# Paired indexer heads, idle products in routing and in the last quarters, and 512-column squares in a one-core transformer block

## The chip, the core and the metric

The kernel runs on one core of a Trainium2 chip. Its engines work side by side and meet at semaphores: PE (TensorE, the matmuls; PEld is its weight loads), DVE (VectorE), ACT (ScalarE), POOL (GpSimd) and SP, which issues the DMAs that bring weights from HBM. The metric is the device time of one execution in microseconds (us).

## The reference, cut to what matters

One layer of 256 frames with 1024 channels: a norm, one wide projection, two attention branches, gates, an output projection, then a mixture of 32 experts and a final norm. Three pieces of it are touched. The **indexer** scores keys with 8 heads of 64 channels:

```python
logits = jnp.einsum('bqhd,bkd->bqhk', qii, k_idx).astype(jnp.float32) * (IDX_DIM ** -0.5)
score = jnp.einsum('bqh,bqhk->bqk', wi.astype(jnp.float32), jax.nn.relu(logits))
_, sel = lax.top_k(score, top_k)          # the keys that branch B attends to
```

The **experts** are 8 groups of 4; each frame goes to one group and two experts in it. The **final norm** closes the block:

```python
for e in range(N_EXPERTS):
    hid = jax.nn.silu(jnp.matmul(h, w_gate[e])) * jnp.matmul(h, w_up[e])
    out = out + jnp.matmul(hid, w_down[e]) * combine[:, e:e + 1]
...
return rmsnorm(x, final_norm_g)
```

## The kernel before, in words

The program is one straight line of stages. **Attention** (to about 218 us) streams 32 slabs of weights through a ring, splits each into a high and a low part on ACT and DVE (L282, L283, L297) and runs three products for each piece on PE (`mm3`, L301 to L303). Up to the output projection a scheduler sets each engine's order, with products of several stages woven into one another. The indexer's scores are made by `select(j)` for the two blocks of 128 queries: block 0 has 128 keys, block 1 has 256. Heads 0 to 3 lie in rows 0 to 63 of the operands, heads 4 to 7 in rows 64 to 127, so each product uses 64 rows of the array (shape 64\*128 in the profile). A bank of PSUM `s` holds 4 heads of block 0 or 2 of block 1; ACT takes the relu (L479), DVE the weighted sum (L482) and the top 64 (L486, L487).

**Routing** (218 to 229 us) and the **experts** (from 229 us) are written in the order in which they run. Routing makes the logits (L778), chooses experts on DVE (`chosen`, L792 to L810), counts places with small products (`cums`, L915, L916, L922), and gathers the tokens (L844). An expert group then takes 12 slabs of 1 MB: two for each expert (`gate_up`, L993) and four quarters of the down projection (`down`, L1030, 256 output channels each). `combine` weighs a result and splits it into `hi` (ACT) and `lo` (DVE), both L297, and its `scatter` adds them with four products (L1044) to the output banks `OA[t][h]`, t for the half of the frames, h for the half of the channels.

Weights of the experts go into some 24 places of SBUF; `take` issues the next DMA when the place's former holder has been used. In the last group (`grp == NG - 1`) `heat` puts idle bf16 products of the identity (L310) after some gate and up products, into a bank `idle_bank` that nobody reads.

The **last quarters** (q = 0 to 3 of the last group) run one by one: `down(q)` calls the scatter of quarter q-1 between its two halves, `combine(q)` follows. Quarters 0 and 1 share one bank of PSUM, 2 and 3 another. After quarter 2 the finished 512 channels are squared (ACT, L318) and multiplied by the norm's gain (DVE, L1112); after quarter 3 the channels 512 to 767 are; the last 256 follow behind the last scatter (L1176), then the roots, the scaling (L1183, L1184) and two DMAs out (L1185).

Of the kernel before, what the change touches and what calls it, by code (L numbers as in the profile page):

```python
# [25 lines left out]
HEAT = 4  # L26
# [52 lines left out]
def block_kernel(ctx: ExitStack, tc: tile.TileContext, a, out, cap=CAP):  # L79
    nc = tc.nc  # L80
# [230 lines left out]

    scr_turn = [0]
# [152 lines left out]
    def select(j):  # L465

        nk = 128 * (j + 1)
        per = 512 // nk
        qs = slice(j * 128, (j + 1) * 128)
        sc = e0[:, 1664:1920] if j else e0[:, 1536:1664]  # L470
        for h0 in range(0, 8, per):
            p = pss()
            for i in range(per):
                h = h0 + i
                ps_ = slice(64 * (h // 4), 64 * (h // 4) + 64)
                mm3(p[:, i * nk:(i + 1) * nk], qiT[ps_, 0, h % 4, qs], qiT[ps_, 1, h % 4, qs],
                    kiT[ps_, 0, :nk], kiT[ps_, 1, :nk], True, True)
            rl = wk.tile([128, 512], F32, tag="b2", name="rl", bufs=3)
            nc.scalar.activation(rl, p, AF.Relu)  # L479
            for i in range(per):  # L480
                h = h0 + i
                nc.vector.scalar_tensor_tensor(sc, rl[:, i * nk:(i + 1) * nk], wi[:, j, h:h + 1],  # L482
                                               adm[:, 256 - nk:] if h == 0 else sc, op0=ALU.mult, op1=ALU.add)
        for r in range(TOPK // 8):
            m8 = wk.tile([128, 8], F32, tag="m8", name="m8")
            nc.vector.max(out=m8, in_=sc)  # L486
            nc.vector.match_replace(out=sc, in_to_replace=m8, in_values=sc, imm_value=TAKEN)  # L487
        nc.vector.tensor_scalar(bias[:, j, :nk], sc, -2e38, NEG, op0=ALU.is_gt, op1=ALU.mult)
# [425 lines left out]
    residual(1)  # L914
    nc.tensor.matmul(cums[0][:, :NE], tri, sel[:, 0], start=True, stop=True)  # L915
    nc.tensor.matmul(cums[1][:, :NE], ones, sel[:, 0], start=True, stop=False)  # L916
    residual(2)
    residual(3)
    in_turn(chosen(1))
    in_turn(placed(0, cums[0][:, :NE]))  # L920
    gx = [pss("gx") for _ in range(2)]
    nc.tensor.matmul(cums[1][:, :NE], tri, sel[:, 1], start=False, stop=True)  # L922
    gather(0, 0, gx[0])
# [98 lines left out]
    def down(grp, q, w, between=None):  # L1022

        if q % 2 == 0:
            Ys[grp, q // 2] = pss("Y")
        Y = Ys[grp, q // 2][:, 256 * (q % 2):256 * (q % 2) + 256]
        wv = w.rearrange("p (f e c) -> p f e c", f=2, e=EPG)
        for f in range(2):
            for e in range(EPG):
                nc.tensor.matmul(Y[quarters[e]], hT_[:, e, f], wv[:, f, e], start=f == 0, stop=f == 1)  # L1030
            if f == 0 and between:
                between()

    def combine(grp, q0, n):
# [4 lines left out]
        evac_g(hi, lo, Ys[grp, h][:, c0:c0 + w], ws)  # L1039

        def scatter():
            for t in range(2):
                for v in (hi, lo):
# [70 lines left out]
    with in_order, tc.manual_schedule(engines={mybir.EngineType.Activation, mybir.EngineType.DVE}):  # L1114
# [42 lines left out]
        scatter = None  # L1157
        for q in range(4):
            down(grp, q, take()[1], scatter)
            scatter = combine(grp, q, 1)  # L1160
            if q == 2:
                for t in range(2):
                    final_part(t, 0, 512, 0)
            elif q == 3:
                for t in range(2):
                    final_part(t, 512, 256, 1)
                nc.vector.tensor_add(fs[:, :, 0], fs[:, :, 0], fs[:, :, 1])
                early = [early_root(fs[:, t, 0:1], D, f"nf{t}") for t in range(2)]
        scatter()
# [3 lines left out]
    with tc.manual_schedule(engines={mybir.EngineType.Activation, mybir.EngineType.DVE}):  # L1173
        cs = slice(768, 1024)
        for t in range(2):
            nc.vector.tensor_mul(ob[:, t, cs], OA[t][1][:, 256:], g_fin[0][:, cs])  # L1176
        roots = []
        for t in range(2):
            sumsq(OA[t][1][:, 256:], 256, fs[:, t, 2:3], scr[:, 2 * t + 1, 256:])
# [90 lines left out]
```

## Time and profile before

| | us |
|---|---|
| three timed runs | 435.72, 432.21, 435.73 (median 435.72) |
| the profiled execution, whole | 431.72 |
| its span, which all times of rows count from | 430.0 |
| PE busy | 397.2 (92%) |
| DVE busy / ACT busy | 206.7 / 184.6 |
| mean granted clock of TensorE over the span | 0.973 |
| DMA read from HBM | 133.36 MB |

All durations in the prediction come from the profiled execution. It stands 4.00 us under the median of the runs and 0.49 us under the fastest of them; the span leaves out 1.72 us of the whole. Views give the start and the duration of an instruction, and neighbours of one kind are merged into one line with a count (x4). Products overlap in the pipeline, so the distance from start to start says what one costs, not its duration. The granted clock is 1.00 at 2.4 GHz and 0.50 at 1.2 GHz.

### The profile page before, as it was taken

The numbers are of one execution on the slowest core, as the hardware profiler recorded it, in microseconds if no ns is written. First come the engines' busy times: TensorE is split into PE (matmuls) and PEld (weight loads), VectorE is DVE, ScalarE is ACT, GpSimd is POOL, SyncE is SP. The second block draws the span as 40 slices with busy tenths as digits, with TensorE's granted clock in tenths as the row PEclk, the third lists the DMA queues.
The fourth block names the chain that finished last, engine by engine and source line by source line (L and its number), as shares of the span: only waits on it lengthen the run. The fifth ranks groups of instructions, "written<-read, shape, count | busy, mean of one in ns | idle before, by whom it ended". The sixth has DMA issues, their size and how long they took to land.

```text
span 430.0 us, 8090 instructions
## 1 busy us (share of the span) xinstructions
PE 397.2 (92%) x3255; PEld 291.6 (68%) x3255; DVE 206.7 (48%) x547; ACT 184.6 (43%) x407; POOL 26.5 (6%) x30
## 2 busy tenths in 40 slices
PE   6999999999999999999989999999999798787760
PEld 3888878888867777888877757575757374364420
DVE  2899599989757464757563221221213011020033
ACT  4885586677756566565433122212221111120242
POOL 0870000000000000000001010101010101000000
PEclk9999999999999999999999999999999979699995
DMA  7985573648543456888994999999999999999952
GB/s 261 390 357 238 196 287 111 257 171 343 197 150 143 148 204 238 325 312 335 332 356 171 425 419 418 422 419 419 420 420 421 419 419 421 421 420 418 414 215 103
DMA packets 20638, 134.98 MB, mean 314 GB/s; under 512 B 2418, under 2 KB 2930, under 8 KB 5620
## 3 DMA queue, kind: packets, MB, share of 16 engines
q1 hardware_dynamic: 20596, 134.42, 79.1%
q8 instruction: 27, 0.44, 0.4%
q14 instruction: 15, 0.12, 0.1%
HBM read 133.36 MB, written 1.05 MB: 313 GB/s over the span
## 4 chain that ended last, share of the span: by engine, by line
PE 70%; DMA 24%; DVE 2%; ACT 1%; issue 0%; SPq 0%; DVEq 0%; ACTq 0%
DMA w<-in_w_moe 23%; PE a L301 13%; PE a L302 13%; PE a L303 12%; PE G L993 8%; PE gx L844 4%; PE Y L1030 3%; PE G L1009 2%; PE OA L1044 2%; PE o L595 2%; PE s L301 2%; PE t L583 1%; PE s L303 1%; PE s L302 1%; DMA w<-in_w_att 1%; PE t L532 1%
## 5 line engine op out<-in xcount | busy, mean ns | idle before, releaser
L302 PE MATMUL a<-r 128*128 128x512 f32 (+1 forms) x244 | 93.7, 388 | 0.0
L303 PE MATMUL a<-r 128*128 128x512 f32 (+1 forms) x244 | 91.9, 383 | 0.0
L301 PE MATMUL a<-r 128*128 128x512 f32 (+1 forms) x244 | 83.7, 387 | 1.0 <-ACT r L297 1.0
L993 PE MATMUL G<-w,tok 128*32 128x256 f32 x1024 | 70.0, 401 | 13.3 <-DMA w<-in_w_moe 13.3
L297 DVE SCALAR_TENSOR_TENSOR r<-w,ident,r 128x512 fp32r<-128x512 f32 (+2 forms) x79 | 62.0, 799 | 13.5 <-ACT r L297 13.3
L297 ACT ACTIVATE r<-w,ident 128x512 fp32r<-128x512 f32 (+2 forms) x79 | 56.6, 751 | 27.4 <-PE a L303 26.2
L993 PEld LDWEIGHTS G<-w,tok 128*32 128x32 f32 x1024 | 29.6, 113 | 39.8 <-issue 15.3
L302 PEld LDWEIGHTS a<-r 128*128 128x128 f32 x244 | 45.9, 188 | 8.6 <-DVE r L297 0.4
L301 PEld LDWEIGHTS a<-r 128*128 128x128 f32 x244 | 44.8, 188 | 10.3 <-ACT r L297 1.9
L303 PEld LDWEIGHTS a<-r 128*128 128x128 f32 x244 | 45.8, 188 | 8.3
L1015 DVE TENSOR_TENSOR P<-G,P 128x64 f32<-128x64 f32 x32 | 7.2, 225 | 82.7 <-ACT P L1014 82.7
L1014 ACT ACTIVATE P<-G 128x64 f32<-128x64 f32 x32 | 7.2, 224 | 75.1 <-PE G L1009 75.1
L1030 PE MATMUL Y<-w,P 128*32 128x256 f32 x512 | 30.5, 382 | 3.2 <-DVE ysb L297 2.2
L999 ACT COPY Gs<-G 128x256 f32<-128x256 f32 x32 | 11.9, 372 | 48.0 <-PE G L993 48.0
L844 PEld LDWEIGHTS gx<-Pr,x 128*128 128x128 f32 x256 | 29.8, 195 | 3.9 <-issue 3.3
L844 PE MATMUL gx<-Pr,x 128*128 128x128 f32 x256 | 31.4, 282 | 0.5 <-DVE Pr L829 0.5
L297 DVE SCALAR_TENSOR_TENSOR ysb<-Y,ws,ysb 128x512 fp32r<-128x512 f32 (+1 forms) x18 | 12.4, 691 | 37.6 <-ACT ysb L297 20.3
L283 DVE TENSOR_TENSOR r<-w,r 128x512 fp32r<-128x512 f32 x32 | 21.9, 690 | 16.7 <-ACT r L282 15.1
L829 POOL TENSOR_SCALAR Pr<-P,r 128x128 f32<-128x128 f32 x14 | 8.3, 607 | 323.5 <-PE gx L844 198.8
L282 ACT CAST r<-w 128x512 fp32r<-128x512 f32 x32 | 19.9, 624 | 14.6 <-PE a L303 9.5
L1030 PEld LDWEIGHTS Y<-w,P 128*32 128x32 f32 x512 | 15.4, 109 | 13.7 <-DVE ysb L297 3.2
L849 DVE TENSOR_TENSOR tok<-gx,ident 128x512 f32<-128x512 f32 x16 | 11.1, 692 | 27.4 <-PE gx L844 27.3
(211 smaller groups left out, 482.2 us busy)
## 6 DMA issues: line engine op xcount, KB each, us to landing
w<-in_w_moe SPq DMA_DIRECT2D x93, 1024.0 KB, 19.8
w<-in_w_att SPq DMA_DIRECT2D x24, 1024.0 KB, 4.9
w<-in_w_moe SPq DMA_DIRECT2D x6, 512.0 KB, 15.0
w<-in_w_att SPq DMA_DIRECT2D x3, 744.0 KB, 8.5
w<-in_w_att SPq DMA_DIRECT2D x2, 512.0 KB, 5.0
out<-r SPq DMA_DIRECT2D x2, 512.0 KB, 3.8
w<-in_w_att SPq DMA_DIRECT2D x1, 768.0 KB, 4.8
w<-in_w_att SPq DMA_DIRECT2D x2, 372.0 KB, 6.1
```

The costliest lines, as they stand in the source:

```text
L282: nc.scalar.copy(hi, src)
L283: nc.vector.tensor_sub(lo, src, hi.bitcast(F32))
L297: return nc.scalar.mul(hi, ps, g), nc.vector.scalar_tensor_tensor(lo, ps, g, hi.bitcast(F32), op0=ALU.mult, op1=ALU.subtract)
L301: i = nc.tensor.matmul(out_, lh, rh, start=start, stop=False)
L302: nc.tensor.matmul(out_, lh, rl, start=False, stop=False)
L303: nc.tensor.matmul(out_, ll, rh, start=False, stop=stop)
L595: nc.tensor.matmul(o[r, c * 256 + 128 * b:(c + 1) * 256], v[:, b, 64 * (4 * quad + h):][:, :64], PT[:, h, 0:2] if b == 0 else PT[:, h, 2], ...
L844: nc.tensor.matmul(p[:, kk * GRP:(kk + 1) * GRP], x2[:, t, k * 128:(k + 1) * 128], Pr[:, t], start=(t == 0 and kk == 0), stop=(t == 1 and ...
L849: nc.vector.tensor_mul(tokens[c], p.rearrange("p (k s) -> p k s", k=4), bc(g_ffn[:, 4 * c:4 * c + 4], GRP, axis=2))
L993: nc.tensor.matmul(G[quarters[2 * z + o], :256], tokens[c][:, kk + o, CAP * e:CAP * e + CAP], w[:, (kk + o) * 512 + z * 256:(kk + o) * 512 ...
L999: nc.scalar.copy(Gs, G[:, :256])
L1030: nc.tensor.matmul(Y[quarters[e]], hT_[:, e, f], wv[:, f, e], start=f == 0, stop=f == 1)
```

## The change

The change has five parts. (1) `select` makes the heads in pairs, one of each half of the rows, and its products alternate between the halves (`mm3_pair`); two banks are filled at once. (2) Routing gets 14 idle products (6, 5 and 3) into the unused columns of `lgp[0]`. (3) In the last four quarters each quarter has a bank of its own, and idle products stand in them: 5 ahead of each scatter, 2 behind each quarter, 10 more ahead of the last scatter; `HEAT`, the number used between gate and up products as well, goes from 4 to 5. (4) `scatter` runs both `hi` products first, then both `lo`. (5) The squares and gain products of channels 512 to 1023 are made in one piece behind the last scatter.

```diff
-HEAT = 4
+HEAT = 5
...
+    row_halves = slice(0, 64), slice(64, 128)
+    def mm3_pair(both, start, stop):
+        for l, r, s0, s1 in ((1, 3, start, False), (1, 4, False, False), (2, 3, False, stop)):
+            for ops in both:
+                nc.tensor.matmul(ops[0], ops[l], ops[r], start=s0, stop=s1)
...
-        for h0 in range(0, 8, per):
-            p = pss()
+        for h0 in range(0, 4, per):
+            p = [pss() for _ in range(2)]
             for i in range(per):
-                h = h0 + i
-                ps_ = slice(64 * (h // 4), 64 * (h // 4) + 64)
-                mm3(p[:, i * nk:(i + 1) * nk], qiT[ps_, 0, h % 4, qs], qiT[ps_, 1, h % 4, qs],
-                    kiT[ps_, 0, :nk], kiT[ps_, 1, :nk], True, True)
-            rl = wk.tile([128, 512], F32, tag="b2", name="rl", bufs=3)
-            nc.scalar.activation(rl, p, AF.Relu)
...
+                mm3_pair([(p[z][:, i * nk:(i + 1) * nk], qiT[ps_, 0, h0 + i, qs], qiT[ps_, 1, h0 + i, qs],
+                           kiT[ps_, 0, :nk], kiT[ps_, 1, :nk]) for z, ps_ in enumerate(row_halves)], True, True)
+            for z in range(2):
+                rl = wk.tile([128, 512], F32, tag="b2", name="rl", bufs=3)
+                nc.scalar.activation(rl, p[z], AF.Relu)
...
     residual(1)
+    heat(lgp[0], 6)
     nc.tensor.matmul(cums[0][:, :NE], tri, sel[:, 0], start=True, stop=True)
...
     residual(3)
+    heat(lgp[0], 5)
...
     nc.tensor.matmul(cums[1][:, :NE], tri, sel[:, 1], start=False, stop=True)
+    heat(lgp[0], 3)
     gather(0, 0, gx[0])
...
-        if q % 2 == 0:
-            Ys[grp, q // 2] = pss("Y")
-        Y = Ys[grp, q // 2][:, 256 * (q % 2):256 * (q % 2) + 256]
+        if q % 2 == 0 or grp == NG - 1:
+            bank = pss("Y")
+            Ys[grp, q] = bank[:, :256]
+            if grp < NG - 1:
+                Ys[grp, q] = bank
+                Ys[grp, q + 1] = bank[:, 256:]
+        Y = Ys[grp, q][:, :256]
...
-            for t in range(2):
-                for v in (hi, lo):
+            for v in (hi, lo):
+                for t in range(2):
...
-        scatter = None
+        def between():
+            heat(idle_bank, HEAT)
+            if scatter:
+                scatter()
+        scatter, idle_bank = None, pt("heat")
         for q in range(4):
-            down(grp, q, take()[1], scatter)
+            down(grp, q, take()[1], between)
+            heat(idle_bank, 2)
             scatter = combine(grp, q, 1)
...
             elif q == 3:
-                for t in range(2):
-                    final_part(t, 512, 256, 1)
-                nc.vector.tensor_add(fs[:, :, 0], fs[:, :, 0], fs[:, :, 1])
                 early = [early_root(fs[:, t, 0:1], D, f"nf{t}") for t in range(2)]
+        heat(idle_bank, 2 * HEAT)
         scatter()
...
-        cs = slice(768, 1024)
-        for t in range(2):
-            nc.vector.tensor_mul(ob[:, t, cs], OA[t][1][:, 256:], g_fin[0][:, cs])
+        cs = slice(512, 1024)
+        for t in range(2):
+            nc.vector.tensor_mul(ob[:, t, cs], OA[t][1], g_fin[0][:, cs])
         roots = []
         for t in range(2):
-            sumsq(OA[t][1][:, 256:], 256, fs[:, t, 2:3], scr[:, 2 * t + 1, 256:])
+            sumsq(OA[t][1], 512, fs[:, t, 2:3], scr[:, 2 * t + 1])
```

The scheduler reweaves the attention stage around the paired products. On PE, in `select(1)` before, the products of the first bank (`s_813`, 256 columns, all on the rows of heads 0 to 3) are broken by transposes (`t`, L532), among products of a projection (`a_883`):

```order
L301 MATMUL a_883<-r_886,r_106 128x512
L301 MATMUL s_813<-r_100,r_99 128x256
L302 MATMUL s_813<-r_100,r_99 128x256
L532 MATMUL t_669<-ident_84,r_103 96x128 x4
L303 MATMUL s_813<-r_100,r_99 128x256
```

Changed, two banks are filled in one unbroken run of twelve, whose line is that of `mm3_pair` (six of them stand here):

```order
L303 MATMUL a_883<-r_886,r_106 128x512
L539 MATMUL t_669<-ident_84,r_103 96x128 x4
L318 MATMUL s_813<-r_100,r_99 128x256
L318 MATMUL s_814<-r_100,r_99 128x256
L318 MATMUL s_813<-r_100,r_99 128x256
L318 MATMUL s_814<-r_100,r_99 128x256
L318 MATMUL s_813<-r_100,r_99 128x256
L318 MATMUL s_814<-r_100,r_99 128x256
```

What moved: neighbours now use different halves of the rows (`s_813` heads 0 to 3, `s_814` heads 4 to 7), and the transposes stand ahead of the run. Next, PE in the last quarter (q = 3) before, with the engines that an instruction waits for:

```order
L1030 MATMUL Y<-w_3543,P 32x256 [waits DMAHW4_49,DVE_49]
L1030 MATMUL Y<-w_3543,P 32x256 x3
L1044 MATMUL OA<-ysb,pl 128x256 [waits Activation_49]
L1044 MATMUL OA<-ysb,pl 128x256 x3
L1030 MATMUL Y<-w_3543,P 32x256 [waits DMAHW5_49]
L1030 MATMUL Y<-w_3543,P 32x256 x3
L1044 MATMUL OA<-ysb,pl 128x256 [waits DVE_49]
L1044 MATMUL OA<-ysb,pl 128x256
```

And changed, from the same product on:

```order
L1044 MATMUL Y<-w_3557,P 32x256 [waits DMAHW4_49,PE_49]
L1044 MATMUL Y<-w_3557,P 32x256 x3
L310 LDWEIGHTS ident_r
L310 MATMUL heat<-ident_r 128x256
...
L1058 MATMUL OA<-ysb,pl 128x256 [waits Activation_49]
L1058 MATMUL OA<-ysb,pl 128x256
L1058 MATMUL OA<-ysb,pl 128x256 [waits DVE_49]
L1058 MATMUL OA<-ysb,pl 128x256
L1044 MATMUL Y<-w_3557,P 32x256 [waits DMAHW5_49]
L1044 MATMUL Y<-w_3557,P 32x256 x3
```

What moved: the quarter no longer waits for DVE, which read the bank that it shared, and five idle products stand ahead of the scatter. Twelve more stand between the last row and the last scatter. Last, DVE behind the last quarter, before:

```order
L297 SCALAR_TENSOR_TENSOR ysb<-Y,ws,ysb 128x256 [waits Activation_49]
L1112 TENSOR_TENSOR r<-OA,g_fin 128x256 [waits Activation_49] x2
L1167 TENSOR_TENSOR fs<-fs 128x2
L326 TENSOR_SCALAR nf0v<-fs 128x1 [waits DVE_49]
L1176 TENSOR_TENSOR r<-OA,g_fin 128x256 [waits PE_49]
```

and changed:

```order
L297 SCALAR_TENSOR_TENSOR ysb<-Y,ws,ysb 128x256 [waits DVE_49,Activation_49]
L334 TENSOR_SCALAR nf0v<-fs 128x1
L335 TENSOR_SCALAR nf0v<-nf0v 128x1 [waits DVE_49]
L334 TENSOR_SCALAR nf1v<-fs 128x1
L335 TENSOR_SCALAR nf1v<-nf1v 128x1 [waits DVE_49]
L1194 TENSOR_TENSOR r<-OA,g_fin 128x512 [waits PE_49] x2
```

What moved: two gain products of 256 columns go from ahead of the last scatter to behind it, where they are one piece with those that stood there.

## Rows read from the trace of the kernel before

**Rows 1.** The page: the granted clock and the DMA share in 40 slices.
```profile
PEclk9999999999999999999999999999999979699995
DMA  7985573648543456888994999999999999999952
```
**Rows 2.** The chain that ended last: start us, us, engine, tile, count.
```profile
301.47 21.19 DMA w<-in_w_moe
...
389.93 18.62 DMA w<-in_w_moe
408.69 1.10 PE Y L1030 x16
```
**Rows 3.** Stretches: us, busy PE, PEld, DVE, ACT, POOL; PEclk, DMA share, GB/s.
```profile
57.00:110.00 53.00, 53.00 (x303) 43.99 (x302) 48.95 (x143) 38.17 (x83) 0.00 (x0) 1.00 0.58 216
222.00:226.00 4.00, 2.64 (x15) 1.76 (x14) 3.52 (x22) 0.00 (x0) 0.00 (x0) 1.00 0.70 289
225.00:230.00 5.00, 4.52 (x46) 4.12 (x49) 3.81 (x19) 1.10 (x6) 1.00 (x2) 1.00 0.03 11
250.00:300.00 50.00, 50.00 (x634) 32.32 (x626) 10.22 (x29) 10.12 (x28) 3.57 (x6) 1.00 1.01 420
340.00:350.00 10.00, 8.25 (x67) 5.04 (x68) 0.26 (x2) 0.97 (x3) 0.00 (x0) 0.66 1.01 420
408.69:420.03 11.34, 7.38 (x79) 3.62 (x80) 4.28 (x13) 4.25 (x14) 0.00 (x0) 1.00 0.49 195
```
**Rows 4.** PE in order of time, block 0 of the indexer: start us, us, instruction.
```profile
59.26 0.27 PE L301 MATMUL s<-r 64*128 64x128 f32 x1
59.37 0.27 PE L302 MATMUL s<-r 64*128 64x128 f32 x1
59.48 0.33 PE L303 MATMUL s<-r 64*128 64x128 f32 x2
59.59 0.33 PE L301 MATMUL s<-r 64*128 64x128 f32 x2
```
**Rows 5.** Stretches of block 1 of the indexer, products of tile `s` alone, columns as above.
```profile
64.38:64.81 0.43, 0.43 (x2) 1.00 0.00 0
65.38:66.75 1.37, 1.36 (x10) 1.00 0.73 102
71.97:73.50 1.53, 1.52 (x12) 1.00 0.00 0
```
**Rows 6.** PE's waits: line, releaser, us in total, times, longest us.
```profile
PE Y L1030 <- DVE ysb L297: 2.2, 2, 1.1
PE OA L1044 <- DVE r L1112: 1.4, 1, 1.4
```
**Rows 7.** In order of time, the last group: start us, us, engine, instruction.
```profile
403.44 0.61 PE L310 MATMUL heat<-ident_r 128*128 128x256 bf16 x4
403.89 0.56 PE L1009 MATMUL G<-cst,Gs 128*128 128x64 f32 x4
...
404.85 1.07 PE L993 MATMUL G<-w,tok 128*32 128x256 f32 x16 [0.40 <-DMA w<-in_w_moe]
...
411.44 0.74 PE L1044 MATMUL OA<-ysb,pl 128*128 128x256 f32 x4
...
412.11 1.07 PE L1030 MATMUL Y<-w,P 128*32 128x256 f32 x16
```
**Rows 8.** The same view, the final norm.
```profile
415.50 0.59 ACT L318 ACTIVATE r<-OA 128x512 f32<-128x512 f32 x1
416.21 1.29 DVE L1112 TENSOR_TENSOR r<-OA,g_fin 128x512 f32<-128x512 f32 x2
...
420.03 0.42 DVE L1176 TENSOR_TENSOR r<-OA,g_fin 128x256 f32<-128x256 f32 x1
...
420.49 0.38 ACT L318 ACTIVATE r<-OA 128x256 f32<-128x256 f32 x1 [1.17 <-DVE r L1176]
```
**Rows 9.** PE in order of time, a product group at the lower clock.
```profile
342.82 1.94 PE L993 MATMUL G<-w,tok 128*32 128x256 f32 x16 [1.50 <-DMA w<-in_w_moe]
```

More of the change, by code (lines that the diff above doesn't have):

```diff
@@ L470, in select @@
         sc = e0[:, 1664:1920] if j else e0[:, 1536:1664]
-        for h0 in range(0, 8, per):
-            p = pss()
+        for h0 in range(0, 4, per):
+            p = [pss() for _ in range(2)]
             for i in range(per):
-                h = h0 + i
-                ps_ = slice(64 * (h // 4), 64 * (h // 4) + 64)
-                mm3(p[:, i * nk:(i + 1) * nk], qiT[ps_, 0, h % 4, qs], qiT[ps_, 1, h % 4, qs],
-                    kiT[ps_, 0, :nk], kiT[ps_, 1, :nk], True, True)
-            rl = wk.tile([128, 512], F32, tag="b2", name="rl", bufs=3)
-            nc.scalar.activation(rl, p, AF.Relu)
[L480 to L483, printed above, removed]
+                mm3_pair([(p[z][:, i * nk:(i + 1) * nk], qiT[ps_, 0, h0 + i, qs], qiT[ps_, 1, h0 + i, qs],
[3 more added lines that the diff above has]
+                nc.scalar.activation(rl, p[z], AF.Relu)
+                for i in range(per):
+                    h = 4 * z + h0 + i
+                    nc.vector.scalar_tensor_tensor(sc, rl[:, i * nk:(i + 1) * nk], wi[:, j, h:h + 1],
+                                                   adm[:, 256 - nk:] if h == 0 else sc, op0=ALU.mult, op1=ALU.add)
         for r in range(TOPK // 8):
@@ L1038, in combine @@
         hi, lo = (wk.tile([128, 512], F32R, tag="b2", name="ysb", bufs=3)[:, :w] for _ in range(2))
-        evac_g(hi, lo, Ys[grp, h][:, c0:c0 + w], ws)
+        evac_g(hi, lo, Ys[grp, q0][:, :w], ws)
         def scatter():
-            for t in range(2):
-                for v in (hi, lo):
+            for v in (hi, lo):
+                for t in range(2):
                     nc.tensor.matmul(OA[t][h][:, c0:c0 + w], pl[:, t * 128:(t + 1) * 128], v, start=False,
```

## Prediction

> **What bounds the kernel now.** I read the page's slices first, then the chain of waits, then a table of stretches, then the order of time in the three places that the change touches. The slices [rows 1] show two regimes: a first half in which the DMA engines have slack, and from about 236 us a DMA share of 9 in every slice almost to the end, with one gap ahead of it: the 4 among the nines, and a share of 0.03 between 225 and 230 us [rows 3]. The clock is full but for two dips and the end.
>
> In the first regime PE sets the pace: between 57 and 110 us it is busy all of the 53.00 us, DVE 48.95 [rows 3]. What PE saves there moves everything behind it. In the second regime the weight stream sets it: the share is 1.01 between 250 and 300 us [rows 3], and the chain is DMA from 301.47 us on [rows 2]. The two are coupled by the gap: the places for expert weights are full, and the stream starts again when the first expert products free them. So an earlier start of the experts shifts the stream's end by as much, as long as the gap of about 5 us is not used up.
>
> The last stage begins when the slab of quarter 0 lands, at 389.93 + 18.62 = 408.55 us; PE starts at 408.69 [rows 2]. From there to the first gain product behind the last scatter at 420.03 [rows 8] PE is busy 7.38 of 11.34 us [rows 3]: short products, then waits for the evacuations (2.2 us for DVE's reading of a shared bank, 1.4 us for DVE's gain products [rows 6]).
>
> **The change, part by part.**
>
> *Paired heads.* Products of one half start 0.11 us apart (59.26, 59.37, 59.48); where the scheduler happened to set the two halves side by side, two start every 0.11 us (59.48, 59.59, each x2) [rows 4]. So a pair costs what one costs, for 128 columns. Of block 0's 24 products 12 stand in such double rows already (six rows, of which two stand here), 12 stand alone: 12 x 0.055 = 0.66 us saved. Block 1's 24 products of 256 columns took 0.43 + 1.36 + 1.52 = 3.31 us, none of them side by side; an unbroken dozen took 1.52 [rows 5]. Twice half of that is 1.52, so 1.79 us are saved. No row shows 256 columns side by side. The ends: only the merging of the broken dozen pays, 0.43 + 1.36 - 1.52 = 0.27 us; or the whole 1.79. I take 1.79, since the nearest row is the same instruction at half the width. Sum 0.66 + 1.79 = 2.4 us, at the low end 0.9. All of it lies on the path, because PE has no idle time there; its cover is DVE, which has 53.00 - 48.95 = 4.05 us to spare [rows 3] and needs 2.4 of them. SP's and POOL's order is unchanged, and the second bank that a pair takes at once is free when its run begins, by the order.
>
> *Routing.* 14 idle products. Four of them took 403.44 to 403.89 us, so 0.11 each [rows 7], 1.5 us in all. PE is idle for 1.36 us between 222 and 226 us, while DVE, which chooses the experts, is busy 3.52 of 4.00 [rows 3]: the idle products lie in waits for DVE, six ahead of the first count, five and three behind it. I cost them at nothing; without that cover they would be 1.5 us, and by the idle time alone 1.5 - 1.36 = 0.2 us stick out. Ends 0 and 0.4.
>
> *HEAT 5 in the last group.* Six more products of 0.11 us, one for each slab; PE waits for the slabs there (0.40 us before the one at 404.85 [rows 7]). Nothing; 0.7 us if PE were behind the stream.
>
> *The scatter's order.* Both `hi` first lets PE start on ACT's result while DVE makes `lo`. In groups 0 to 6 the stream hides it. In the last quarters idle products stand ahead of it, and by then both are there. Nothing.
>
> *The last quarters.* The banks of their own remove the 2.2 us of waits, and the gain products' 1.4 us wait goes with the squares; but 38 idle products (4 x 5, 4 x 2 and 10) of 0.11 us bring 4.2 us to PE. They go into 11.34 - 7.38 = 3.96 us of idle time. Walked through: four quarters at 1.0 (404.85 to the idle products 1.0 later, and 1.07 for the sixteen at 412.11), three scatters at 0.67 (411.44 to 412.11) [rows 7], 4.2 of idle products, some 0.5 of change-overs, then three products of the last scatter, 0.5: 408.69 + 4.0 + 2.0 + 4.2 + 0.5 + 0.5 = 419.9, against 420.03. So what was late for waiting is now late for idle products: PE becomes the bound of the tail and the freed banks pay nothing. I take 0. Ends: -0.6 without change-overs; +1.5 if each idle product costs its share of the group's whole duration, 0.61 / 4 = 0.15 us.
>
> *Squares in one piece.* Behind the last scatter the gain product grows from 0.42 to 1.29 / 2 = 0.65 us, and the square, which waits for it, from 0.38 to 0.59 [rows 8]: 0.23 + 0.21 = 0.4 us longer for the first half of the frames, and the second follows it. What stood ahead of the scatter and goes was waited for, but that wait is counted above. +0.4; ends 0.2 and 0.65 (if the second square adds its own 0.21).
>
> **The sum.** The profiled execution took 431.72 us (span 430.0). 431.72 - 2.4 + 0 + 0 + 0 + 0.4 = **429.7 us**. That is 2.5 us under the fastest timed run and 6.0 us under the median. The difference between these two is the second question: the runs lie at two levels, 432.21 and twice 435.72, with the profiled execution at the lower. In the profile the clock falls to its lower level twice; between 340 and 350 us its mean is 0.66, which is 6.8 us at 0.50 [rows 3], and sixteen products took 1.94 us there against 1.07 [rows 7, 9]. Both dips lie under the stream and cost nothing. A dip of 6.8 us where PE sets the pace would cost about half of itself, 3.4 us, and the levels are 3.5 us apart. That the upper level is such a dip in routing or in the tail is argued, not shown. The idle products raise PE's use in just those places (2.64 of 4.00 busy in routing, 7.38 of 11.34 in the tail [rows 3]), so my forecast has the median of the changed kernel at the lower level.
>
> **The rivals.**
>
> *A: the pairs pay nothing, or DVE takes it back.* DVE's 1.65 us that would be left of its slack are little over a woven order; a PE that waits for it loses what the pairs won. 431.72 + 0.4 = 432.1 us, 431.2 with the low end of 0.9. For it: DVE at 92% [rows 3]. Against: the double rows [rows 4]. The double rows also speak on a rule of the Trainium skill: page "TensorE: Matmul & The Clock Gate", section "LDWEIGHTS (loading the stationary operand)", times a weight load by its columns, P / 1.2 ns, whatever the rows. By an estimate from it each 128-column load takes 0.107 us, 48 loads in a row would set the pace as before, and the sum would be 432.1; the trace has two products with a load each in 0.11 us, which does not agree. Chance 0.15.
>
> *B: the upper level stays.* If the idle products don't keep the clock up, or the level is of another origin (the weight stream's rate), most runs stay 3.5 us higher: 433.2 us. For it: two of three runs, and nothing in this trace shows the cause. Against: the size fits. The same page of the Trainium skill, section "Why this matters for your kernels", blames a fallen clock on idle gaps between bursts of products. By that rule routing, whose 1.36 us of idle time [rows 3] come in pieces between products, needs no idle products and 433.2 would stand; in this trace the clock was low at 342.82 with a wait of only 1.50 us ahead of the products [rows 9], so a long gap is not what it took. Chance 0.25.
>
> *C: slower.* The tail now hangs on PE alone, 7.38 + 4.2 = 11.6 us of it. If the clock is low when quarter 0 lands and stays low, each product takes 1.94 / 1.07 = 1.8 times as long: 0.8 x 11.6 = 9.4 us, 439.1 us. It decides against the change from 6.0 us on, that is if the clock is low for 7.5 of the 11.6 us. Against: the last group's idle products kept it at 1.00 in the profile [rows 3]. Chance 0.04.
>
> *D: better.* The tail's low end and a woven order that suits: 428.7 us. Chance 0.06.
>
> **How the numbers follow.** The forecast keeps 0.50, with a range of its own from 429.0 to 431.2 (the low end of the pairs). The range from 428.6 to 433.9 takes in A, most of B and D. About 1% is what a measurement of this kernel can tell from no change; against the median of 435.72 that is 431.36 and 440.08. Faster: forecast and D, 0.56. Slower: the upper half of C, 0.03. The same: 0.41.
>
> **What would show it.** Right: double rows all through the indexer's products, with block 1's dozens in about 0.8 us; the first gather and the landing of quarter 0's slab about 2.4 us earlier; no idle time of PE over 0.3 us in the last quarters, idle products up to the last scatter, which ends 11.3 us after that landing; about 0.4 us more from there to the end; clock 1.00 in routing and tail in every execution. Wrong: block 1's products still 0.12 us apart, PE waiting for DVE before 110 us (A); runs at two levels (B); a clock of 0.50 behind 406 us (C); or a last scatter that ends much sooner, idle products hidden.

## The result

| | before | after |
|---|---|---|
| median of 12 timed runs, us | 434.57 | 430.70 |
| fastest and slowest of them | 431.55, 436.13 | 429.29, 432.48 |
| the profiled execution, whole | 431.72 | 429.82 |
| its span | 429.95 | 428.04 |

The ratio is 0.9924, with a 95% interval from 0.9896 to 0.9951: 0.8% faster, within the 1% that the prediction counts as no change. The forecast was 429.7 us, with a range from 428.6 to 433.9. The sum forecast 2.0 us for one undisturbed execution; the two traces differ by 1.91 us. The medians differ by 3.87 us; where the other 2.0 us come from is not shown (last bullet of the part on the prediction). One run of the kernel before, beside the y kernels, took 452.66 us at a mean granted clock of 0.849 and is left out of all ranges and spreads below.

**Profile after.** All line numbers here are those of the changed kernel: it has 7 to 18 lines more than before, so L1044 is what was L1030 (Y), L1058 what was L1044 (OA), L1003 what was L993 (G), L851 what was L844 (gx), L1194 the final gain product, L1201 the final scaling, L318 now `mm3_pair`. First the page's slices of after, to be held against [rows 1]:

```profile
PEclk9999999999999999999999999999999989799996
DMA  7996574556643464979875999999999999999942
```

The two regimes stand as before; the gap of the weight stream, one digit of 4 before, is a 5 in the same slice now.

The order of time on PE in the indexer of after (start us, us, instruction), against [rows 4]. Block 0 first, then block 1's two dozens:

```profile
57.20 0.44 PE L318 MATMUL s<-r 64*128 64x128 f32 x4
58.66 1.33 PE L318 MATMUL s<-r 64*128 64x128 f32 x20
64.46 0.98 PE L318 MATMUL s<-r 64*128 64x256 f32 x12
70.36 0.98 PE L318 MATMUL s<-r 64*128 64x256 f32 x12
```

Then the stretches of after, from the start of a run of pairs to the start of the next product, tile `s` alone (us, busy PE and count, PEld, DVE, ACT, granted clock, DMA share, GB/s), against [rows 5]:

```profile
58.66:59.92 1.26, 1.26 (x20) 1.19 (x20) 0.00 (x0) 0.00 (x0) 1.00 0.97 384
64.46:65.38 0.92, 0.92 (x12) 0.78 (x12) 0.00 (x0) 0.00 (x0) 1.00 0.36 71
70.36:71.26 0.90, 0.90 (x12) 0.76 (x12) 0.00 (x0) 0.00 (x0) 1.00 0.00 0
```

Of block 0, which [rows 4] show only in part, the same stretches of before are (us, busy PE and count, granted clock, DMA share, GB/s):

```profile
57.28:57.65 0.37, 0.36 (x4) 1.00 1.00 421
58.76:60.74 1.98, 1.98 (x20) 1.00 1.03 426
```

A dozen of block 1 took 1.52 us unpaired and takes 0.92 and 0.90 now. Block 0's twenty took 1.98 us and take 1.26; they start 1.26 / 20 = 0.063 us apart, alone they stood 0.11 apart. The pairs run side by side at 256 columns too, which no row of before showed.

What that is worth is read between two marks on PE: a set of four transposes (`t`) that stands ahead of all the indexer's work, and the first gather of tokens behind it. The rows of before, then those of after:

```profile
46.11 0.60 PE L510 MATMUL t<-ident,r 128*128 128x128 f32 x4
225.66 3.84 PE L844 MATMUL gx<-Pr,x 128*128 128x128 f32 x32 [0.48 <-DVE Pr L829]
229.43 1.93 PE L993 MATMUL G<-w,tok 128*32 128x256 f32 x32
```

```profile
45.99 0.60 PE L517 MATMUL t<-ident,r 128*128 128x128 f32 x4
223.03 3.84 PE L851 MATMUL gx<-Pr,x 128*128 128x128 f32 x32 [0.15 <-DVE Pr L836]
226.80 2.80 PE L1003 MATMUL G<-w,tok 128*32 128x256 f32 x48
```

Before, 225.66 - 46.11 = 179.55 us; after, 223.03 - 45.99 = 177.04: 2.51 us less. From the gather to the first gate product it is 3.77 us in both. PE waits 0.15 us for DVE ahead of the gather in place of 0.48; the last three idle products stand in the difference.

The stretches of after that answer to [rows 3]:

```profile
57.00:110.00 53.00, 53.00 (x322) 43.73 (x321) 49.80 (x145) 39.34 (x85) 0.00 (x0) 1.00 0.60 228
222.00:226.00 4.00, 3.85 (x34) 3.41 (x32) 2.91 (x19) 1.10 (x6) 0.61 (x1) 1.00 0.17 66
225.00:230.00 5.00, 5.00 (x69) 3.52 (x68) 2.15 (x8) 0.37 (x1) 1.21 (x2) 1.00 0.16 46
250.00:300.00 50.00, 50.00 (x635) 32.95 (x635) 9.29 (x27) 10.30 (x29) 3.16 (x6) 1.00 1.01 420
406.07:417.50 11.43, 11.43 (x118) 6.46 (x118) 3.82 (x12) 3.50 (x10) 0.00 (x0) 1.00 0.47 190
```

PE is still busy all of the 53 us in the indexer's stretch, DVE 49.80 of them: it has taken up the faster pace and is not yet the bound. In the last quarters PE was busy 7.38 of 11.34 us and is busy 11.43 of 11.43 now. The chain that ended last (start us, us, engine, tile) says it in another way, against [rows 2]:

```profile
387.22 18.71 DMA w<-in_w_moe
406.07 0.64 PE Y L1044 x8
406.70 0.65 PE heat L310 x5
...
415.12 0.57 PE Y L1044 x8
415.69 1.42 PE heat L310 x12
417.50 0.70 DVE r L1194
```

Idle products stand in the chain itself, the last twelve for 1.42 us. PE's waits (releaser: us in total, times, longest) had 2.2 us of Y for DVE and 1.4 us of OA for DVE [rows 6]; both are gone, and of Y's only this is left:

```profile
PE Y L1044 <- DMA w<-in_w_moe: 0.7, 1, 0.7
```

The final norm, against [rows 8]; the first fence is the rest of before, which closes with DVE's second scaling, the second is after:

```profile
423.20 0.55 DVE L1183 TENSOR_SCALAR r<-r,rf 128x640 f32<-128x640 f32 x1
```

```profile
417.50 1.29 DVE L1194 TENSOR_TENSOR r<-OA,g_fin 128x512 f32<-128x512 f32 x2 [0.26 <-PE OA L1058]
418.22 0.60 ACT L326 ACTIVATE r<-OA 128x512 f32<-128x512 f32 x1 [2.00 <-DVE r L1194]
...
421.15 0.55 DVE L1201 TENSOR_SCALAR r<-r,rf 128x640 f32<-128x640 f32 x1
```

From the first final gain product to the second scaling: 3.17 us before, 3.65 after. From there to the end, where the last transfer goes out: 6.75 and 6.89.

### The profile page after: what moved, and what is told of

Read it like the earlier page. It is cut to its first block, busy times and chain, and to the rows that moved or that the text cites. A ratio compares the mean times of both kernels' runs of the same rounds, so it can differ in the third digit from the quotient of the medians.

```text
span 428.0 us, 8201 instructions
## 1 busy us (share of the span) xinstructions
PE 399.8 (93%) x3313; PEld 294.2 (69%) x3313; DVE 206.0 (48%) x544; ACT 184.0 (43%) x403; POOL 26.4 (6%) x30
## 4 chain that ended last, share of the span: by engine, by line
PE 76%; DMA 19%; DVE 2%; ACT 1%; issue 0%; SPq 0%; DVEq 0%; ACTq 0%
DMA w<-in_w_moe 18%; PE a L301 13%; PE a L302 13%; PE a L303 12%; PE G L1003 9%; PE gx L851 5%; PE Y L1044 5%; PE OA L1058 3%; PE G L1019 3%; PE o L602 2%; PE t L590 1%; PE heat L310 1%; PE s L301 1%; DMA w<-in_w_att 1%; PE s L302 1%; PE s L303 1%
## 5 line engine op out<-in xcount | busy, mean ns | idle before, releaser
L1003 PE MATMUL G<-w,tok 128*32 128x256 f32 x1024 | 68.7, 395 | 13.9 <-DMA w<-in_w_moe 13.9
L1003 PEld LDWEIGHTS G<-w,tok 128*32 128x32 f32 x1024 | 29.3, 111 | 39.5 <-issue 14.6
L851 PEld LDWEIGHTS gx<-Pr,x 128*128 128x128 f32 x256 | 30.7, 200 | 4.1 <-issue 3.7
L851 PE MATMUL gx<-Pr,x 128*128 128x128 f32 x256 | 32.2, 286 | 0.2 <-DVE Pr L836 0.2
L1044 PE MATMUL Y<-w,P 128*32 128x256 f32 x512 | 30.7, 382 | 0.7 <-DMA w<-in_w_moe 0.7
L1019 PEld LDWEIGHTS G<-cst,Gs 128*128 128x128 f32 x128 | 17.1, 195 | 9.3 <-issue 4.9
```

What stands on the lines that cost most here:

```text
L851: nc.tensor.matmul(p[:, kk * GRP:(kk + 1) * GRP], x2[:, t, k * 128:(k + 1) * 128], Pr[:, t], start=(t == 0 and kk == 0), stop=(t == 1 and ...
L1003: nc.tensor.matmul(G[quarters[2 * z + o], :256], tokens[c][:, kk + o, CAP * e:CAP * e + CAP], w[:, (kk + o) * 512 + z * 256:(kk + o) * 512 ...
L1019: nc.tensor.matmul(HT[:, f * 64:(f + 1) * 64], Gs[:, f * 128:(f + 1) * 128], fold, start=True, stop=True)
```

## The experiments

All kernels were profiled once and timed in 6 or 12 runs beside the kernel before. The table cuts each profiled execution at the same marks: (a) start of the four transposes, (b) from there to the first gather, (c) to the first gate product, (d) to the first product of quarter 0's slab in the last group, (e) to the first final gain product, (f) to the second scaling on DVE, (g) to the span's end. A row adds up to its span.

| kernel | a | b | c | d | e | f | g | runs: median (fastest to slowest), n | ratio [95%] |
|---|---|---|---|---|---|---|---|---|---|
| before | 46.11 | 179.55 | 3.77 | 179.26 | 11.34 | 3.17 | 6.75 | 434.57 (431.55 to 436.13), 12 | |
| after | 45.99 | 177.04 | 3.77 | 179.27 | 11.43 | 3.65 | 6.89 | 430.70 (429.29 to 432.48), 12 | 0.9924 [0.9896, 0.9951] |
| x0 before again | 47.84 | 179.56 | 3.77 | 179.26 | 11.32 | 3.18 | 6.26 | 433.22 (431.17 to 436.13), 12 | 0.9997 [0.9966, 1.0028] |
| x1 pairs only | 49.20 | 177.07 | 5.39 | 179.34 | 11.32 | 3.17 | 6.53 | 431.85 (428.33 to 433.80), 12 | 0.9937 [0.9904, 0.9970] |
| x2 no idle tail | 46.41 | 177.00 | 3.77 | 179.23 | 9.76 | 3.65 | 6.22 | 428.32 (427.81 to 430.43), 6 | 0.9885 [0.9839, 0.9932] |
| x3 no idle routing | 47.68 | 177.00 | 3.77 | 179.37 | 11.43 | 3.65 | 6.94 | 431.36 (429.57 to 434.21), 12 | 0.9950 [0.9914, 0.9985] |
| y1 warm start | 46.56 | 177.04 | 3.77 | 180.30 | 11.43 | 3.65 | 6.90 | 431.24 (429.38 to 432.80), 12 | 0.9955 [0.9926, 0.9983] |
| y2 split squares | 47.43 | 177.03 | 3.77 | 179.67 | 10.61 | 3.17 | 6.64 | 429.56 (427.91 to 430.31), 12 | 0.9905 [0.9877, 0.9932] |
| y3 routing idle only | 47.49 | 179.60 | 3.77 | 179.16 | 11.34 | 3.17 | 6.26 | 433.90 (430.96 to 437.20), 12 | 1.0012 [0.9978, 1.0047] |
| y4 all | 46.76 | 177.01 | 3.77 | 179.21 | 10.56 | 3.17 | 6.65 | 429.77 (428.91 to 431.36), 12 | 0.9921 [0.9893, 0.9949] |
| z1 no idle tail again | 48.53 | 177.07 | 3.77 | 179.32 | 9.72 | 3.65 | 7.07 | 429.79 (427.68 to 430.90), 6 | 0.9901 [0.9863, 0.9940] |
| z2 split squares again | 48.32 | 177.04 | 3.77 | 179.26 | 10.54 | 3.16 | 6.81 | 428.69 (427.66 to 430.77), 6 | 0.9887 [0.9847, 0.9927] |
| z3 no pairs | 45.89 | 179.55 | 3.77 | 179.15 | 9.76 | 3.64 | 6.78 | 431.25 (430.01 to 432.12), 12 | 0.9952 [0.9929, 0.9975] |
| z4 scatter order | 48.31 | 177.04 | 3.77 | 179.09 | 9.76 | 3.65 | 6.77 | 429.13 (427.74 to 430.63), 6 | 0.9892 [0.9850, 0.9933] |

Columns b, e and f repeat within 0.1 us wherever the code is the same, so they price an edit far more finely than the medians can; a and g wander by 3.3 and 0.85 us whatever the kernel, and d by 0.6 us, 1.2 with y1. Before again is also the measure of how much a median of 12 may wander.

### The kernel before once more

> The kernel before, unchanged, run against itself. Ratio 1.00 within 0.4%. Question: what tells an execution of 432 us from one of 435.7 us. Theory of the clock (a dip where PE sets the pace): the longer executions show a lower mean granted clock, by about 3.4 us / 432 us x 0.5 or more, so 0.973 in the short ones and about 0.965 in the long ones. Rival (the weight stream or something else sets the length): the mean clock doesn't fall with the length.

Ratio 0.9997. It has the same b to f as the first profile; what differs is a, 1.73 us later, and g, 0.49 us less. The question on the clock has half an answer. Over the 92 runs of the kernel before in all experiments, the 21 under 432.3 us have a mean granted clock of 0.981 and the rest 0.974, the same at 433 us as at 436. So a lower clock goes with the step away from the shortest runs, as the theory has it, and not with the length beyond it; the section on the start shows that this record can miss a low clock.

### What the pairs are worth

x1 is the kernel before with the pairs alone; z3 has everything but the pairs and the idle products of the tail (the diff is that of the change's indexer, forward and back):

```diff
-            for i in range(per):
-                mm3(p[:, i * nk:(i + 1) * nk], ...
+            for i in range(per):
+                mm3_pair([(p[z][:, i * nk:(i + 1) * nk], ...) for z, ps_ in enumerate(row_halves)], True, True)
```

> The kernel before with the paired heads alone. My theory: first gather at 225.66 - 2.6 = 223.0 us, quarter 0's slab 2.6 us earlier, tail as before (11.3 us from its first product to the first gain product behind the last scatter, then 9.9 us), so the profiled execution at 431.7 - 2.6 = 429.1 us and the same spread of executions as before: ratio 0.994. Rival (the pairs also take away what makes the long executions): ratio about 0.990, executions within 3 us of one another. Rival (the idle products alone make the difference in the medians): ratio 0.997 or more.

> The changed kernel without the idle products of the last quarters and without the pairs: what is left is routing's idle products, the banks of their own, squares in one piece and the scatter's order. Theory (pairs are worth 2.5 us, whatever else is changed): 2.3 to 2.7 us above the kernel with the pairs in the median; and between two marks that lie ahead of and behind the indexer on PE, 2.5 us longer. Rival (a part of it is given back later): under 2 us. On the spread of the runs: the kernels with both routing's idle products and the new last quarters had 2.4 to 3.4 us, those with one or none of the two 4.6 to 6.2; if these two make the spread, it is under 3.4 us here; if the pairs had a part in it, over 4 us.

Column b is 179.55 to 179.60 us in the four kernels without pairs and 177.00 to 177.07 in the ten with them: 2.5 us, whatever else is changed. The runs of x1 agree: its ratio is worth 434.23 x 0.0063 = 2.7 us (434.23 was the median of before beside it), and x1's spread, 5.5 us, is no smaller than before's. Its profiled execution took 433.80 us where 429.1 was expected: 3.09 us of the difference are column a, 1.62 are column c. Neither comes with the pairs as such: x3, which has them too and no idle products in routing, has 47.68 and 3.77. For z3 the runs decide nothing: its median is 1.46 us above z1's (under 2, as the rival has it) and 2.12 above z4's, with 6 runs of each of these and spreads of 3 us. By the traces nothing of the pairs is given back, for the columns c to f add up to 196.32 us in z3 and 196.46 in z1. x1's ratio, 0.9937, and that of the whole change, 0.9924, have intervals that overlap: in the runs the other four parts cannot be told from nothing.

### Idle products and squares in the last quarters

x2 and z1 are the changed kernel without the idle products there; y2 and z2 have in addition the squares of channels 512 to 767 ahead of the last scatter, as before; z4 is x2 with the scatter's old order.

```diff
         def between():
-            heat(idle_bank, HEAT)
...
             down(grp, q, take()[1], between)
-            heat(idle_bank, 2)
...
-        heat(idle_bank, 2 * HEAT)
         scatter()
```

> The changed kernel without the idle products of the last four quarters (banks of their own, HEAT 5 between gate and up products, routing's idle products and the late squares stay). My theory says that with them PE is the bound of the tail: without them the tail is paced by the landing of the slabs, and the first gain product behind the last scatter comes 9.5 us behind quarter 0's first product instead of 11.4; profiled execution 429.8 - 1.9 = 427.9 us, if the clock stays at 1.00 there. Rival (the idle products keep the clock up in the tail): a clock of 0.50 somewhere in the last quarters, tail not shorter than 11.4 us in the profile or in most executions, median 431 us or more.

Column e falls from 11.43 to 9.76 us, and the granted clock stays at 1.00 through the last scatter, by the stretch of x2 (columns as above, POOL after ACT):

```profile
406.41:416.17 9.76, 7.73 (x80) 3.76 (x80) 3.81 (x13) 3.50 (x10) 0.00 (x0) 1.00 0.57 227
```

So 38 idle products cost 1.67 us and guard nothing that a trace shows. The 9.76 us are near the 9.5 of the theory, and it is right on what sets them: where PE waited twice for DVE's reading of the shared banks (2.2 us [rows 6]), it now waits for the slabs. The first products of quarters 2 and 3 in x2, 2.50 us apart:

```profile
410.25 0.64 PE L1044 MATMUL Y<-w,P 128*32 128x256 f32 x8 [0.59 <-DMA w<-in_w_moe]
412.75 0.64 PE L1044 MATMUL Y<-w,P 128*32 128x256 f32 x8 [0.62 <-DMA w<-in_w_moe]
```

Put the squares back (y2):

```diff
             elif q == 3:
+                for t in range(2):
+                    final_part(t, 512, 256, 1)
+                nc.vector.tensor_add(fs[:, :, 0], fs[:, :, 0], fs[:, :, 1])
...
-        cs = slice(512, 1024)
+        cs = slice(768, 1024)
```

> The changed kernel without the idle products of the last quarters, and with the squares and gain products of channels 512 to 767 ahead of the last scatter as in the kernel before. Theory (squares in one piece cost 0.4 to 0.6 us behind the last scatter): from the first final gain product to the span's end 9.9 to 10.0 us in place of 10.5 (9.87 in the trace with no idle products and squares in one piece counts against that: there the part from 416.17 to 426.04 took 9.87, so the split should give 9.3 to 9.5). Rival (the whole difference lies in how the last output transfer falls): the final part stays at 9.9 us. By a second theory the early work on DVE and ACT stands in the way of the last quarters' evacuations and the stretch from quarter 0's first product to the first final gain product grows from 9.76 us to 10.3 or more, which takes the gain back.

The second theory held: e is 10.61 us, 0.85 more than x2, f is 3.17, 0.48 less. The last scatter of y2, and then of x2, in order of time:

```profile
417.08 0.75 DVE L1126 TENSOR_TENSOR r<-OA,g_fin 128x256 f32<-128x256 f32 x2
417.55 1.13 PE L1058 MATMUL OA<-ysb,pl 128*128 128x256 f32 x4 [1.45 <-DVE r L1126]
418.51 0.76 DVE L1194 TENSOR_TENSOR r<-OA,g_fin 128x256 f32<-128x256 f32 x2 [0.17 <-PE OA L1058]
```

```profile
415.23 1.02 PE L1058 MATMUL OA<-ysb,pl 128*128 128x256 f32 x4 [0.59 <-ACT ysb L297]
416.17 1.29 DVE L1191 TENSOR_TENSOR r<-OA,g_fin 128x512 f32<-128x512 f32 x2
```

The scatter is due to write OA while DVE's early gain product still reads it, and waits 1.45 us for DVE; in x2 it waits 0.59 us, for ACT's `hi`. This is the wait of [rows 6] on OA, so it goes with the squares, not with the banks. The runs were to settle it on one chip:

> The changed kernel without the idle products of the last quarters once more, beside the split squares and on the same chip. In the traces so far the stretch from the last quarter's last product to the first final gain product took 2.18 us here and 3.05 us with the split squares, where the last scatter waits 1.45 us for DVE's early gain product, which reads the bank that the scatter writes. Theory (the squares of channels 512 to 767 ahead of the last scatter block it): this kernel is 0.4 to 0.9 us under the split one in the median, ratio to the kernel before 0.988. Rival (the two traces differ by chance): the medians of the two are equal within 0.3 us.

> The split squares once more, beside the kernel with squares in one piece on the same chip. Theory (the early gain product blocks the last scatter): 0.4 to 0.9 us above that one in the median, and the wait of about 1.45 us of the last scatter for DVE stands in this trace too. Rival (chance): equal within 0.3 us.

The traces repeat: e and f together are 13.37 us in z1 and 13.70 in z2, and z2's last scatter has the wait again:

```profile
418.05 0.97 PE L1058 MATMUL OA<-ysb,pl 128*128 128x256 f32 x4 [1.45 <-DVE r L1126]
```

But the gain is 0.33 to 0.37 us net, less than the 0.4 to 0.9 expected, and the medians stand the other way round: 429.79 and 428.69, with 6 runs each and spreads of 3 us. So that squares in one piece are better by a third of a microsecond is read from the traces, and the timed runs neither show nor refute it.

> The changed kernel without the idle products of the last quarters, and with the scatter's old order: hi and lo of the first half of the frames, then of the second. I gave the order no price, because idle products stood ahead of it. Theory (without them the last scatter starts on ACT's result 0.5 us before DVE's is there, and the old order waits behind its first product): from the last quarter's last product to the first final gain product 2.3 to 2.5 us in place of 2.18, the median 0.1 to 0.3 us above; in groups 0 to 6 nothing. Rival: no difference within 0.1 us.

```diff
-            for v in (hi, lo):
-                for t in range(2):
+            for t in range(2):
+                for v in (hi, lo):
```

The rival held: e is 9.76 us in both orders. The price of 0 was right, and it did not need the idle products that the prediction gave as its reason.

### Routing's idle products

x3 takes the 14 out of the changed kernel, y3 puts them alone into the kernel before:

```diff
     residual(1)
-    heat(lgp[0], 6)
...
     residual(3)
-    heat(lgp[0], 5)
...
-    heat(lgp[0], 3)
     gather(0, 0, gx[0])
```

> The changed kernel without routing's 14 idle products. My theory: they lie in waits for DVE and cost nothing, so in an execution without a dip nothing changes (profiled 429.8 us, first gather at 223.0 us). If they keep the clock up, part of the executions is longer by some 3 us: median 432 to 433 us, with a lower mean clock in the long ones. Rival (they do nothing): same median and spread as the changed kernel, ratio to the kernel before 0.992.

> The kernel before with routing's 14 idle products alone. My prediction gave them no price in an undisturbed execution: the stretch from the first gathered frames to the first gate product stays at 3.77 us, profiled 431.7 us where the clock rises at the start as early as in the profile of before. Theory (they keep the clock from falling to half in routing, which cost 1.6 us in the trace of the pairs alone): the upper end of the runs falls by about 1.6 us, the median by 0.5 to 1.5 us. Rival (nothing): median and spread as the kernel before in the same job, ratio 0.999 to 1.001. Other rival (they stick out): 0.2 to 0.4 us longer, the ratio 1.001.

They cost at most 0.05 us (b: 177.04 against 177.00, 179.60 against 179.55). In the runs x3's median is 0.66 us above after's and its spread 4.6 us against 3.2, between theory and rival, and the intervals of the two overlap; its three longest runs, 433.04 to 434.21 us, show mean clocks of 0.979 to 0.983, so the lower clock of the theory is not seen in them. What they may buy was seen once: in x1, which has none, column c is 5.39 in place of 3.77. The stretches of x1 around it, with PE's row:

```profile
222.00:226.00 4.00, 2.91 (x15) 1.92 (x14) 3.45 (x22) 0.36 (x1) 0.00 (x0) 1.00 0.86 340
226.00:230.00 4.00, 3.73 (x18) 3.73 (x19) 2.26 (x16) 1.10 (x6) 0.00 (x0) 0.57 0.08 35
230.00:234.00 4.00, 4.00 (x60) 2.91 (x62) 1.38 (x2) 0.34 (x1) 1.20 (x2) 1.00 0.14 18
```

```profile
226.27 5.46 PE L851 MATMUL gx<-Pr,x 128*128 128x128 f32 x32 [0.48 <-DVE Pr L836]
231.66 1.71 PE L1000 MATMUL G<-w,tok 128*32 128x256 f32 x27
```

The clock was at its lower level for most of the gathers, right behind the stretch in which PE had been busy 2.91 of 4.00 us: 1.62 us lost. The kernel before runs the same products there with the same wait of 0.48 us, was busy 2.64 of 4.00 us and kept 1.00 [rows 3], so these rows do not tell when the clock falls. One of the four profiled kernels without these products shows it, none of the ten with them. But y3 did not lower the long executions (437.20 us was its slowest; ratio 1.0012), so this dip alone is not what makes them.

### The start

The transposes of column a start anywhere between 45.89 and 49.20 us in kernels with the same start, 3.3 us apart, and b repeats. Most of the difference arises in the first 16 us. The same four products of 512 columns there, before, then x1:

```profile
10.45 0.40 PE L301 MATMUL a<-r 128*128 128x512 f32 x1
10.69 0.39 PE L302 MATMUL a<-r 128*128 128x512 f32 x1
...
12.49 0.40 PE L302 MATMUL a<-r 128*128 128x512 f32 x1
12.72 0.39 PE L303 MATMUL a<-r 128*128 128x512 f32 x1
```

```profile
11.94 0.65 PE L301 MATMUL a<-r 128*128 128x512 f32 x1
12.39 0.63 PE L302 MATMUL a<-r 128*128 128x512 f32 x1
...
15.30 0.40 PE L302 MATMUL a<-r 128*128 128x512 f32 x1
15.53 0.39 PE L303 MATMUL a<-r 128*128 128x512 f32 x1
```

x1 is 1.49 us behind at the first of them and 2.81 at the third, of the 3.09 us by which column a differs; 0.59 us stand already ahead of it, at the first transposes (4.84 and 5.43 us). Before's products start 0.23 to 0.24 us apart; x1's stand 0.45 apart at 11.94 us and 0.23 at 15.30, which is the ratio of the two levels of the clock. The granted clock itself is no witness for x1: it is 1.00 in its row of this stretch. In that of x0, which is the kernel before, it is 0.50. One microsecond of x0, then of x1 (columns as in [rows 3]):

```profile
11.00:12.00 1.00, 1.00 (x5) 0.81 (x5) 0.88 (x2) 0.23 (x1) 0.00 (x0) 0.50 1.06 432
11.00:12.00 1.00, 1.00 (x5) 0.81 (x5) 0.46 (x1) 1.00 (x2) 0.00 (x0) 1.00 1.07 435
```

So a low clock in x1 is inferred from the spacing. In x0 the clock was 1.00 from 9 to 10 us, 0.50 from 11 to 13 and 1.00 again from 14 on, with the same pair of products 0.45 us apart (10.70 and 11.15 us). The Trainium skill (page "TensorE: Matmul & The Clock Gate", section "What's actually happening") says that the point of rise differs from run to run of one kernel; the traces of before and x0, one kernel, agree in that the clock was full at 11 us in one and at half in the other, though in x0 it had risen once and fallen again. y1 has eight idle products in place of five ahead of the first norm, and 1 and 5 in place of 0 and 2 behind the first transposes; y4 has that, no idle products in the tail, and the split squares:

```diff
-    for _ in range(5):
+    for _ in range(8):
         nc.tensor.matmul(p, zeros[:, :128], zeros, start=True, stop=True)
...
-            if t == 0 and q == 1:
-                for _ in range(2):
+            if t == 0:
+                for _ in range((1, 5)[q]):
```

> The changed kernel with more idle products at the start only: a loop over zeros of 8 turns in place of 5 ahead of the first norm, and 1 and 5 idle products behind the first half's transposes in place of 0 and 2. Theory (the spread of executions comes from how early the clock becomes full at the start, seen from 7.0 to 14.7 us in the traces so far, and from a dip in routing): the clock is full by about 8 us in every execution, the runs' spread falls from 3.2 us to under 2 us, and the median is 429.5 us or less, 0.7 to 1.5 us under the changed kernel's in this job; profiled span 427.0 to 428.0 us. Rival (the spread is of another origin, or the granted clock does not follow these products): the spread stays at 3 us or more, and the median is the same or up to 0.5 us above, for the added products.

> The changed kernel with three edits: no idle products in the last quarters, the squares of channels 512 to 767 ahead of the last scatter, and more idle products at the start. If each pays what its theory says (1.7 us, 0.4 us, about 1 us in the median), the median is 426.5 to 427.5 us and the ratio to the kernel before 0.982 to 0.985; if only the tail's idle products pay, 428.3 us as that kernel measured, ratio 0.988.

The rival held. The clock was full early in both traces, as the theory has it (products 0.24 us apart from 8.91 us in y1, from 9.07 in y4), and column a is early (46.56, 46.76), but before, after, x2 and z3 were as early without it. y1's runs spread over 3.4 us, as after's do, and its median is not lower; y4's median is 0.2 us above y2's, and its 429.77 us are above both values that were expected. If the rise comes earlier on average, it is by less than these runs can tell. y1's d is 0.6 to 1.2 us longer than the others'; nothing in this edit touches that stretch, and its cause is not known.

**The best of them** is the changed kernel without the idle products of the last quarters (x2, z1): 428.32 and 429.79 us, ratios 0.9885 and 0.9901, against 0.9924 for the change. y2 and z2, with the split squares, are as good by the runs (0.9905, 0.9887). The intervals of all these overlap with that of the change; that the idle products of the last quarters should go rests on column e.

## Why the prediction was right, and where not

- *Pairs, -2.4 us:* right. Measured -2.51. Block 1 gave 3.33 - 1.82 = 1.5 of it, where 1.79 was forecast: a dozen takes 0.91 us and not half of 1.52. Block 0 gave (0.37 + 1.98) - (0.36 + 1.26) = 0.73, where 0.66 was forecast. The 0.27 that are left by subtraction lie in the new weave, and no row shows which wait or gap gave them. They make up for what block 1 fell short of, so that the sum came out is in part luck. Rival A fell: DVE is busy 49.80 of 53 us and PE does not wait. By the rule that a load takes its columns / 1.2 ns (the Trainium skill, page "TensorE: Matmul & The Clock Gate", section "LDWEIGHTS (loading the stationary operand)"), an estimate for twelve loads of 128 columns is 1.28 us; the dozen with its twelve loads took 0.90 to 0.92, so for loads into alternating halves of the rows the measurement decides.
- *Routing, 0, HEAT 5, 0, scatter order, 0:* right, within 0.05 us for routing (columns b and c) and for the scatter's order (z4). HEAT 5 was not tried by itself: d is 179.26 and 179.27, but d wanders by 0.6 us.
- *Last quarters, 0:* right in sum (+0.09) and in its reason. Without idle products the stretch is 9.76 us, so banks and squares had won 1.58, and the idle products took 1.67 back. The parts differ from the working: own banks are worth 11.34 - 10.61 = 0.73 us (y2) and not the 2.2 us of waits, because PE then waits for the slabs instead (0.59 and 0.62 us); the squares are worth 0.85 and not 1.4, because the last scatter then waits 0.59 us for ACT. Rival C did not come: the granted clock was 1.00 from quarter 0's slab to the last scatter in the trace, and no run came near 439 us.
- *Squares, +0.4:* measured +0.48 behind the scatter. That what stood ahead of it was waited for is shown by z2 and y2.
- *The last transfer:* not in the sum; +0.14, and it varies by 0.85 us from execution to execution.
- *The median at the lower level:* this step failed. I took the runs of before for two levels, 3.5 us apart, and expected the changed kernel at the lower one. There are no levels: the runs of the kernel before in all its timings fill the range from 430.63 to 436.31 us with no gap over 0.3, and those of after lie from 429.29 to 432.48. Up to 3.3 us of a run can come from the start (column a), which the change does not touch. So the median came out at 430.70 and not at 429.7, while the fastest run fell by 2.3 us, close to the 2.0 of the sum, and the slowest by 3.7. Rival B did not come either: no run of after reached its 433.2 us. And the median of three runs, 435.72, was 1.1 us above that of twelve: it was the height of the sample, no level.
- *What stays open:* kernels that have both routing's idle products and the new last quarters spread over 2.1 to 3.4 us, some of them in 6 runs only (after, x2, y1, y2, y4, z1, z2, z3, z4), those with one or none of the two over 4.3 to 6.2 (before in each of its timings, x0, x1, x3, y3). The pairs have no part in it (z3: 2.1). A fallen clock in routing was seen to lengthen one execution (x1), but routing's idle products alone did not narrow the spread (y3: 6.2); in the last quarters no profiled execution of the old ones shows one, and only one execution of each kernel was profiled. The cause there is not shown, and with it the 2.0 us by which the median fell more than the traces are not explained.

## What to carry to other kernels

Price an edit between two marks of the trace that bracket it, and not by the median: here the marks repeated within 0.1 us, while executions of one kernel lay 3 to 6 us apart. Two products that use different halves of the rows belong next to each other. Idle products are free only where a wait is sure to cover them: routing's 14 stood in waits for DVE and cost nothing, 38 in the last quarters filled the room that the freed banks and the late squares had made, and the same time was lost to them instead. And a wait that goes may uncover the next: of 2.2 us of waits for a shared bank 0.73 were gained, because the slabs came next.

## What was not expected of the hardware

- Products of 64 rows and 256 columns pair like those of 128 columns, at 0.91 / 1.52 = 0.60 of the time (128 columns: 0.063 / 0.11 = 0.57), each with a weight load of its own.
- What happens in the first 16 us moved the whole rest of the program by up to 3.3 us (45.89 to 49.20 us at the same instruction). By the spacing of the products a low clock is the larger part of it in x1, and the record of the granted clock can stand at 1.00 while products start at half their pace (x1 at 11.94 us). Two kernels with more idle products there did not show a lower median.
- From the start of the last scaling to the end, with the same two output DMAs, it took 6.22 to 7.07 us.
